# Layer 0's convolution stage of a two-layer diffusion trunk: a list scheduler's order on all engines, other tap numbers on GpSimd, seven projection tiles at other places

## The chip, the cores and the metric

The kernel runs on one core of a Trainium2 chip. The metric is the device time of one execution in microseconds (us); lower is better. Five queues run side by side and meet only at semaphores: TensorE (PE in the profile, its weight loads PEld), VectorE (DVE), ScalarE (ACT), GpSimd (POOL), and SyncE (SP), which here issues nearly all DMAs. Each works through its own instructions strictly in the order in which the program lists them: an instruction that waits holds up all that stand behind it on the same engine.

## The reference, cut to what matters

One inference step on 128 context tokens and 512 latent tokens (640 columns in the kernel, laid out with the channels on the partitions). Layer 0 is a Conformer convolution branch, layer 1 a bidirectional state-space branch. The change touches layer 0 alone:

```python
def conformer_branch(h, on_grid, w_in, b_in, w_dw, b_dw, ln_g, ln_b, w_out):
    u = h @ w_in + b_in
    a, a_gate, z = jnp.split(u, 3, axis=-1)
    v = a * jax.nn.sigmoid(a_gate)
    ...                                     # latent tokens: rows of 64 columns, each padded by itself
    v = depthwise_conv(v, w_dw, b_dw)       # 31 taps, padding 15
    v = jax.nn.silu(layer_norm(v, ln_g, ln_b))
    return (v * jax.nn.silu(z)) @ w_out
```

`w_in` is 1024 x 6144, so `a`, `a_gate` and `z` have 2048 channels each: 16 tiles of 128 channels each, 48 tiles in all. All arithmetic is in float32.

## The kernel before, in words

**Projection.** A tile of `u` is 128 channels by 640 columns in one PSUM buffer of two banks, 320 columns each. Each weight tile `wf` (512 KB) is split into a rounded part `wh` (ScalarE, L78) and the rest `wl` (GpSimd, L80), and so is the activation (`h_hi`, `h_lo`); a tile is the sum of three products over eight blocks of 128 inputs and two halves, 48 matmuls (`dense_all`, L157). There are two PSUM buffers for these products (`mm`), two buffers for `wf` and three each for `wh` and `wl`. Tiles are named a0 to a15, g0 to g15 (the gate) and z0 to z15 below. g0, a0 and g1 are made while the input is normalised; from 57 us on the stage makes a1, then g2, a2, g3, a3 and so on, z0 to z6 between them, and after the convolutions z7 to z15. In the profile a tile is called `u__` and a number: u__609 is a1, u__3811 is z6.

**Gate and convolution.** ScalarE takes the sigmoid of a g tile (L333), VectorE multiplies (L338, `v`). Item i of the convolution is channel tile i of `v`. Its centre tap is made by ScalarE into an accumulator `cva` in PSUM (L354, two of them), and 30 taps are left. Most are one VectorE instruction each (L361); the outermost ones, which are the shortest, are made by ScalarE as a product `tp` (L385, three buffers) that GpSimd adds (L390) to `cv`, the item's result in SBUF, once ScalarE has copied the accumulator there (L388). The context tokens are treated as two rows of 64 as well, and GpSimd adds what crosses the seam between them (L375, L377, L394). How many taps of an item go to ScalarE and GpSimd is a tuple of 16 numbers, 94 taps in all. For items 14 and 15 `cv` is cleared first and VectorE adds the accumulator last (L392).

**Sums beside it.** The layer norm needs the sums of `cv` and of its square over all channels. For items 0 to 9 they are made in a third kind of product, `side` (L190), which takes one of the two `mm` buffers, six items behind the gate; VectorE adds them up (L402). Items 10 to 15 go into one PSUM buffer `pst` later, and the statistics follow (L502 to L518). In the same `side` buffer 12 blocks of the adaLN parameters are multiplied (L111, weights `wa`, four DMAs of 256 KB per block), copied as a row by ScalarE (L117) and turned by TensorE in the spare columns of the next a tile (L122).

**After it.** z7 to z15 are multiplied, VectorE normalises the 16 items (L524, L525), gates them (L530), and the output projection `o` follows in three passes; layer 1 begins behind it.

**What sets the order.** In layer 0 the framework decides: it keeps the written order as a priority and issues on each engine what its own model of readiness lets it. Layer 1 has a list scheduler written in the kernel, the class `Order`: generators yield operations with an engine and a planned duration, keys (results) and rings (buffers), and `run` always issues the operation that can start earliest by its own clocks. Planned durations set the order and nothing else; on the chip the engines wait for semaphores.

Of the kernel before, what the change touches and what calls it, by code (L numbers as in the profile page):

```python
# [13 lines left out]
P = 128  # L14
NT = 640
# [26 lines left out]
def trunk(ctx: ExitStack, tc: tile.TileContext, a: dict):  # L42
# [190 lines left out]

    first = {}
# [57 lines left out]
    with tc.tile_pool(name="l0", bufs=1) as lp:  # L292
# [5 lines left out]
        LAG = 10  # L298


        Z_AT = {5: (0,), 10: (1,), 13: (2,), 14: (3, 4), 15: (5, 6)}
        Z_END = list(range(7, 16))
# [3 lines left out]
        order += [32 + j for j in Z_END]  # L306

# [23 lines left out]
        def sigmoid(i, psg):  # L331
            sg = tmp.tile([P, NT], F32, tag="tm", bufs=2, name="sg")
            S.activation(out=halves(sg), in_=psg[:, :, 0:HN], func=AF.Sigmoid, bias=c("b_in", 16 + i))  # L333
            return sg

        def gate(i, sg, psa):
            v = tmp.tile([P, NT], F32, tag="v", bufs=4, name="v")
            V.scalar_tensor_tensor(out=halves(v), in0=psa[:, :, 0:HN], scalar=c("b_in", i), in1=halves(sg), op0=ALU.add, op1=ALU.mult)  # L338
            return i, v

# [6 lines left out]
        def conv(items, npool, final=False):  # L347


            order = sorted((t for t in range(CK) if t != 15), key=lambda t: -abs(t - 15))  # L350
            late, taps = order[:npool], order[npool:]
            accs = [cvp.tile([P, 1024], F32, tag="cva", bufs=2, name="cva")[:, 0:NT] for _ in items]
            for (i, v), acc in zip(items, accs):
                S.activation(out=acc, in_=v, func=AF.Identity, scale=w_dw(i, 15), bias=c("b_dw", i))  # L354
                if final:
                    G.memset(cv[i], 0.0)
            for tap in taps:
                d = tap - 15
                lo, hi = max(0, -d), min(64, 64 - d)
                for (i, v), acc in zip(items, accs):  # L360
                    V.scalar_tensor_tensor(out=rows(acc)[:, :, lo:hi], in0=rows(v)[:, :, lo + d : hi + d], scalar=w_dw(i, tap), in1=rows(acc)[:, :, lo:hi], op0=ALU.mult, op1=ALU.add)  # L361
            for (i, v), acc in zip(items, accs):
                out = cv[i]

                e = eb[i % 3]
                S.copy(out=e[:, 0, 14:29], in_=v[:, HN : HN + 15])
                S.copy(out=e[:, 1, 0:15], in_=v[:, 49:64])
                oa = out[:, 49:64]
                seam = bass.AP(tensor=oa.tensor, offset=oa.offset, ap=[list(oa.ap[0]), [HN - 49, 2], [1, 15]])
                ea = e[:, :, :]  # L370
                win = bass.AP(tensor=ea.tensor, offset=ea.offset, ap=[list(ea.ap[0]), [30, 2], [1, 15], [1, 15]])
                wa = w_dw(i, 16)
                wv = bass.AP(tensor=wa.tensor, offset=wa.offset, ap=[list(wa.ap[0]), [-16, 2], [1, 15], [0, 15]])
                pr = lp.tile([P, 2, 15, 15], F32, tag="pr", bufs=1, name="seam")
                G.tensor_tensor(out=pr, in0=win, in1=wv, op=ALU.mult)  # L375
                for a0, a1, n in ((0, 8, 7), (0, 4, 4), (0, 2, 2), (0, 1, 1)):
                    G.tensor_add(out=pr[:, :, a0 : a0 + n, :], in0=pr[:, :, a0 : a0 + n, :], in1=pr[:, :, a1 : a1 + n, :])  # L377
                if final:
                    G.tensor_add(out=seam, in0=seam, in1=pr[:, :, 0, :])
                tps = []  # L380
                for tap in late:
                    d = tap - 15
                    lo, hi = max(0, -d), min(64, 64 - d)
                    tp = lp.tile([P, 10, 52], F32, tag="tp", bufs=3, name="tp")
                    S.activation(out=tp[:, :, 0 : hi - lo], in_=rows(v)[:, :, lo + d : hi + d], func=AF.Copy, scale=w_dw(i, tap))  # L385
                    tps.append((tp, lo, hi))
                if not final:
                    S.copy(out=out, in_=acc)  # L388
                for tp, lo, hi in tps:
                    G.tensor_add(out=rows(out)[:, :, lo:hi], in0=rows(out)[:, :, lo:hi], in1=tp[:, :, 0 : hi - lo])  # L390
                if final:
                    V.tensor_add(out=out, in0=out, in1=acc)  # L392
                else:
                    G.tensor_add(out=seam, in0=seam, in1=pr[:, :, 0, :])  # L394

        def ln_sums(i, ps):
            sq = tmp.tile([P, NT], F32, tag="tm", bufs=2, name="sq")
            S.activation(out=sq, in_=cv[i], func=AF.Square)
            for t, s in ((cv[i], 0), (sq, QN)):
                quarter_sums(ps[:, s : s + QN], t, True, True)  # L400
            if i:
                V.tensor_add(out=ssum, in0=ssum, in1=ps[:, 0 : 2 * QN].rearrange("p (a n) -> p a n", a=2))  # L402
# [1268 lines left out]
```

## Time and profile before

| | us |
|---|---|
| median of 3 runs | 1117.86 (1117.59 to 1118.91) |
| the profiled execution's own time | 1117.72 |
| its span, first to last instruction | 1115.9 |
| projection and convolution, a1 to z6 on TensorE | 57.2 to 368.5 |
| last addition of the convolution on VectorE | 387.8 |
| sums of items 10 to 15 added up | 396.6 |
| first output pass on TensorE ends | 471.4 |

The page gives the busy time of each engine and the costliest groups. The views used below: the windows (busy time of each engine between two times), the groups (engine, operation, `out<-in`, shape, count, busy time, mean of one, idle time before them and what ended it), the waits (who waited for whom, total, times, longest), the timeline (start, length, engine, line, and in brackets the idle time before and its releaser) and the chain of work that ended last (start, length, what). Matmuls overlap: a tile of 48 issues every 7.04 us.

### The profile page before, as it was taken

The numbers are of one execution on the slowest core, as the hardware profiler recorded it, in microseconds if no ns is written. First come the engines' busy times: TensorE is split into PE (matmuls) and PEld (weight loads), VectorE is DVE, ScalarE is ACT, GpSimd is POOL, SyncE is SP. The second block draws the span as 40 slices with busy tenths as digits, with TensorE's granted clock in tenths as the row PEclk, the third lists the DMA queues.
The fourth block names the chain that finished last, engine by engine and source line by source line (L and its number), as shares of the span: only waits on it lengthen the run. The fifth ranks groups of instructions, "written<-read, shape, count | busy, mean of one in ns | idle before, by whom it ended". The sixth has DMA issues, their size and how long they took to land.

```text
span 1115.9 us, 19084 instructions
## 1 busy us (share of the span) xinstructions
PE 1067.5 (96%) x7560; PEld 971.8 (87%) x7560; DVE 831.1 (74%) x1182; ACT 573.4 (51%) x994; POOL 493.3 (44%) x421
## 2 busy tenths in 40 slices
PE   6999999998998999899999999999999999999996
PEld 3898889797898999899989897899899888978896
DVE  2579999989899859623368978998766695777673
ACT  6544456455645356421266666584536472644442
POOL 1255797788778726600000046414541544254213
PEclk9999999999999999999999999999999999999997
DMA  9434224323321211432412274334343514343102
GB/s 362 166 118 147 95 95 133 111 85 126 101 68 60 77 48 38 146 110 67 142 40 95 72 156 117 87 103 115 86 115 104 118 63 114 104 114 87 57 20 94
DMA packets 79049, 115.95 MB, mean 104 GB/s; under 512 B 26096, under 2 KB 49008, under 8 KB 78960
## 3 DMA queue, kind: packets, MB, share of 16 engines
q1 hardware_dynamic: 78240, 113.91, 34.4%
q8 instruction: 59, 0.97, 0.4%
q10 hardware_dynamic: 720, 0.82, 0.2%
q14 instruction: 30, 0.25, 0.1%
HBM read 109.80 MB, written 4.92 MB: 103 GB/s over the span
## 4 chain that ended last, share of the span: by engine, by line
PE 71%; DVE 14%; ACT 6%; issue 3%; DMA 3%; POOL 1%; SPq 1%; POOLq 0%; DVEq 0%; ACTq 0%
PE pz L833 8%; PE o L833 8%; PE xs L833 6%; DVE cva L361 3%; PE o L1342 3%; PE po L1114 2%; PE pst L1051 2%; PE B L833 2%; PE py L1182 2%; DVE xs L875 2%; DVE cn L524 2%; ACT wh L78 2%; PE C L833 1%; PE o__5398 L148 1%; PE o__4929 L148 1%
## 5 line engine op out<-in xcount | busy, mean ns | idle before, releaser
L361 DVE SCALAR_TENSOR_TENSOR cva<-v,cst,cva 128x550 f32<-128x550 f32 (+12 forms) x386 | 286.0, 815 | 10.2 <-ACT cva L354 8.7
L80 POOL TENSOR_TENSOR wl<-wf,wh 128x1024 fp32r<-128x1024 f32 (+1 forms) x50 | 119.1, 2382 | 122.2 <-ACT wh L78 117.4
L78 ACT CAST wh<-wf 128x1024 fp32r<-128x1024 f32 (+1 forms) x75 | 71.5, 956 | 180.0 <-PE o__4929 L148 37.4
L390 POOL TENSOR_TENSOR cv<-cv,tp 128x490 f32<-128x490 f32 (+3 forms) x94 | 113.4, 1211 | 14.1 <-ACT cv L388 9.4
L795 ACT CAST wh<-wf 128x1024 fp32r<-128x1024 f32 x53 | 55.5, 1047 | 82.1 <-PE o L833 27.8
L799 DVE TENSOR_TENSOR wl<-wf,wh 128x1024 fp32r<-128x1024 f32 x51 | 69.2, 1357 | 32.9 <-ACT wh L795 32.4
L833 PE MATMUL o<-yhl,wh 128*128 128x320 f32 x384 | 92.1, 327 | 0.0
L385 ACT ACTIVATE tp<-v,cst 128x490 f32<-128x490 f32 (+3 forms) x94 | 65.8, 716 | 40.6 <-POOL cv L390 40.5
L833 PE MATMUL pz<-h_hi,wh 128*128 128x384 f32 (+1 forms) x256 | 84.6, 330 | 0.5 <-ACT up L862 0.5
L1120 POOL TENSOR_TENSOR y<-y,yo 128x512 f32<-128x512 f32 x32 | 44.7, 1397 | 80.9 <-DVE yo L1118 80.8
L833 PE MATMUL pz<-h_hi,wl 128*128 128x384 f32 (+1 forms) x256 | 79.1, 309 | 0.0
L833 PE MATMUL pz<-h_lo,wh 128*128 128x384 f32 (+1 forms) x256 | 79.0, 309 | 0.0
L833 PE MATMUL xs<-h_hi,wh 128*128 128x384 f32 (+1 forms) x224 | 77.4, 346 | 0.0
L80 DVE TENSOR_TENSOR wl<-wf,wh 128x512 fp32r<-128x512 f32 (+1 forms) x25 | 27.2, 1087 | 66.3 <-ACT wh L78 66.2
L833 PEld LDWEIGHTS o<-yhl,wh 128*128 128x128 f32 x384 | 63.9, 188 | 7.8 <-issue 7.8
L875 DVE SCALAR_TENSOR_TENSOR xs<-up,cst,xs 128x642 f32<-128x642 f32 x64 | 69.0, 1079 | 2.2 <-ACT xs L873 0.8
L833 PE MATMUL xs<-h_hi,wl 128*128 128x384 f32 (+1 forms) x224 | 69.3, 309 | 0.0
L833 PE MATMUL xs<-h_lo,wh 128*128 128x384 f32 (+1 forms) x224 | 69.2, 309 | 0.0
L833 PE MATMUL o<-yhl,wl 128*128 128x320 f32 x192 | 59.2, 309 | 0.0
L989 POOL TENSOR_TENSOR gb<-gb,cols 128x512 f32<-128x512 f32 x20 | 24.9, 1246 | 75.8 <-DMA gb<-acd 75.8
L995 ACT ACTIVATE gf<-gf,cols 128x128 f32<-128x128 f32 x160 | 49.8, 392 | 16.6 <-DVE gf L991 16.5
L628 POOL MEMSET up<- 128x2 f32 x2 | 0.2, 100 | 117.2 <-DVE h_lo L219 117.2
(685 smaller groups left out, 3406.7 us busy)
## 6 DMA issues: line engine op xcount, KB each, us to landing
wf<-w_in SPq DMA_DIRECT2D x48, 512.0 KB, 3.6
wa<-w_ada SPq DMA_DIRECT2D x64, 256.0 KB, 4.8
wf<-w_out SPq DMA_DIRECT2D x24, 512.0 KB, 3.7
wf<-w_xbc SPq DMA_DIRECT2D x24, 512.0 KB, 3.7
gf<-acd SPq DMA_DIRECT2D x40, 256.0 KB, 4.8
wa<-w_ada SPq DMA_DIRECT2D x16, 512.0 KB, 10.2
wf<-w_z SPq DMA_DIRECT2D x16, 512.0 KB, 3.8
gb<-acd SPq DMA_DIRECT2D x40, 128.0 KB, 4.7
```

The source lines that it names most:

```text
L78: S.copy(out=wh[:, :n], in_=wf[:, :n])
L80: sub.tensor_sub(out=wl[:, :n], in0=wf[:, :n], in1=wh[:, :n].bitcast(F32))
L361: V.scalar_tensor_tensor(out=rows(acc)[:, :, lo:hi], in0=rows(v)[:, :, lo + d : hi + d], scalar=w_dw(i, tap), in1=rows(acc)[:, :, lo:hi], ...
L385: S.activation(out=tp[:, :, 0 : hi - lo], in_=rows(v)[:, :, lo + d : hi + d], func=AF.Copy, scale=w_dw(i, tap))
L390: G.tensor_add(out=rows(out)[:, :, lo:hi], in0=rows(out)[:, :, lo:hi], in1=tp[:, :, 0 : hi - lo])
L795: S.copy(out=cell["wh"], in_=cell["wf"])
L799: e_.tensor_sub(out=cell["wl"], in0=cell["wf"], in1=cell["wh"].bitcast(F32))
L833: T.matmul(ps[:, b, at_ : at_ + t1 - t0], lhsT=w_, rhs=t_[:, t0:t1], start=k == 0 and n == 0, stop=k == nk - 1 and n == 2)
L875: t = yield op(VL, 0.89, lambda: V.scalar_tensor_tensor(out=acc, in0=u[:, d : d + PW], scalar=c("w_c", j * 5 + d), in1=acc, op0=ALU.mult, ...
L995: t = yield op(ACT, 0.39, lambda: S.activation(out=gv[:, h_, :], in_=gv[:, h_, :], func=AF.Exp, bias=cols1[ch][:, o8 + h_ : o8 + h_ + 1]), ...
L1120: t = yield op(PO, 1.29, lambda: G.tensor_add(out=y, in0=y, in1=yo))
L1342: T.matmul(ps, lhsT=wt, rhs=t_[:, tok], start=k == 0 and n == 0, stop=k == 3 and n == 2)
```

## The change

The class `Order` moves ahead of layer 0 unchanged but for its priorities, which it now takes as an argument, and layer 0's stage is written as generators for it. `PLAN0` is TensorE's order of a, g, z and side products (`s`); `NPOOL` the numbers of taps that go to ScalarE and GpSimd, 121 in all. Sums stand in the side product of their number, behind the ada block and ahead of the next a tile. Weight loads and the loads of the ada blocks are issued in the scheduler's order. The split of the first weight tile in `PLAN0` may go to VectorE and does; all others go to GpSimd. The buffer `tp` gets 54 columns a row instead of 52. The work itself is the same: 36 tiles in this stage, 12 blocks, 10 items' sums, 30 taps an item.

```diff
-        Z_AT = {5: (0,), 10: (1,), 13: (2,), 14: (3, 4), 15: (5, 6)}
-        order = [1]
-        for i in range(16):
-            order += [18 + i, 2 + i] * (i < 14) + [32 + j for j in Z_AT.get(i, ())]
...
-            conv([items[i]], (7, 6, 7, 6, 7, 6, 7, 6, 7, 6, 7, 6, 6, 4, 3, 3)[i], i >= 14)
...
+        PLAN0 = "a1 g3 s3 g2 s2 z0 a2 a3 z1 g5 g4 s4 s5 a4 a5 g6 s6 a6 g7 s7 a7 g8 s8 g9 a8 z2 z3 s9 a9 g10 s10 a10 g11 s11 a11 g12 s12 a12 g13 s13 a13 g14 s14 a14 g15 s15 a15 z4 z5 z6"
+        NPOOL = (10, 7, 9, 7, 6, 9, 11, 5, 4, 7, 10, 10, 10, 8, 4, 4)
...
+        def weights():
+            for m in tiles0 + order[:2]:
+                yield get("wf")
+                wf = gp.tile([P, 1024], F32, tag="wf", bufs=2, name="wf")
+                t = yield op(SP, 0.35, lambda: nc.sync.dma_start(out=wf, in_=a["w_in1"][m]))
+                start(split(m, wf), t)
+
+        def split(m, wf):
+            yield get("wh")
+            wh = gp.tile([P, 1024], F32R, tag="wh", bufs=3, name="wh")
+            yield op(ACT, 1.05, lambda: S.copy(out=wh, in_=wf))
+            yield get("wl")
+            wl = gp.tile([P, 1024], F32R, tag="wl", bufs=3, name="wl")
+            t = yield either((PO, 2.41, lambda: G.tensor_sub(out=wl, in0=wf, in1=wh.bitcast(F32))), (VL, 1.23, lambda: V.tensor_sub(out=wl, in0=wf, in1=wh.bitcast(F32))), bias=0.0 if m == tiles0[0] else 9.0)
...
+        def blocks():
+            for n, (l, b) in enumerate(BLOCKS):
+                if n > 1:
+                    yield key(("ada", n - 2))
+                for _ in range(4):
+                    yield get("cs")
+                blk = []
+                t = yield op(SP, 1.8, lambda: blk.append(ada_load(l, b, cs, 2)))
...
+        def filler():
+            blks = []
+            for name in plan:
+                i = int(name[1:])
+                if name[0] == "s":
+                    n = i - 2
...
+                    yield get("mm")
+                    ps = mm("side")
+                    if n < 12:
...
+                        t = yield op(PE, 1.07, sums_of_block)
...
+                    if i >= 6:
+                        j = i - 6
+                        yield key(("sq", j))
...
+                        t = yield op(PE, 0.78, sums)
...
+        def conv():
+            for i in range(16):
+                yield key(("init", i))
+                for tap in TAPS[NPOOL[i]:]:
+                    d, lo, hi = span_of(tap)
+                    t = yield op(VE, 0.24 + 0.01 * (hi - lo), lambda: V.scalar_tensor_tensor(out=rows64(accs[i], lo, hi), in0=rows64(vs[i], lo + d, hi + d), scalar=w_dw(i, tap), in1=rows64(accs[i], lo, hi), op0=ALU.mult, op1=ALU.add))
+                post(("taps", i), t)
+                start(copied(i), t) if i < 14 else start(last_add(i), t, "conv")
...
+        def seam_sums(i):
...
+            for n, tap in enumerate(TAPS[:NPOOL[i]]):
+                d, lo, hi = span_of(tap)
+                yield key(("tp", i, n))
+                t = yield op(PO, 1.12 if i < 14 else 1.3, lambda: G.tensor_add(out=rows64(cv[i], lo, hi), in0=rows64(cv[i], lo, hi), in1=sgs["tp", i, n][:, :, 0 : hi - lo]))
+                put("tp", t)
...
+        with tc.manual_schedule():
+            run.clock = [0.0, -3.0, -3.0, -3.0, -9.0]
...
+            start(weights(), -9.0)
+            start(after_g(0, first[0][1]), -1.8)
+            start(after_g(1, first[2][1]), 0.0)
+            start(blocks(), -9.0)
+            start(filler(), 0.0)
```

How it moves instructions, at the places that the prediction speaks of. **SyncE's queue as the stage begins**: `wf` are the weight tiles of `w_in`, the first of them a1's; `wa` with 1024 columns are the last blocks for the stage ahead, `wa` with 512 columns those of the side products, whose buffers lie where the stage ahead had its own. Before:

```order
L76 DMA wf_597<-w_in1 128x1024
L104 DMA wa_444<-w_ada 128x1024
L104 DMA wa_446<-w_ada 128x1024
L76 DMA wf_603<-w_in1 128x1024
L76 DMA wf_660<-w_in1 128x1024
L104 DMA wa_718<-w_ada 128x512
L104 DMA wa_720<-w_ada 128x512
L104 DMA wa_722<-w_ada 128x512
L104 DMA wa_724<-w_ada 128x512
L76 DMA wf_726<-w_in1 128x1024
```

Now:

```order
L104 DMA wa_444<-w_ada 128x1024
L104 DMA wa_446<-w_ada 128x1024
L104 DMA wa_592<-w_ada 128x512
L104 DMA wa_594<-w_ada 128x512
L104 DMA wa_596<-w_ada 128x512
L104 DMA wa_598<-w_ada 128x512
L470 DMA wf_589<-w_in1 128x1024
L104 DMA wa_603<-w_ada 128x512
L104 DMA wa_605<-w_ada 128x512
L104 DMA wa_607<-w_ada 128x512
L104 DMA wa_609<-w_ada 128x512
L470 DMA wf_601<-w_in1 128x1024
```

a1's weights stood ahead of the last loads of the stage before; they stand now behind the first four loads of the side blocks.

**ScalarE at the same place**: `u__253` is g0, `u__254` g1, `wh` a weight tile's rounded part. Before:

```order
L333 ACTIVATE sg<-u__253,cst_92 128x640
L78 CAST wh<-wf 128x1024 x2
L333 ACTIVATE sg<-u__254,cst_92 128x640
L366 COPY eb_581<-v 128x15
L367 COPY eb_581<-v 128x15
L385 ACTIVATE tp<-v,cst_92 128x10x49 x2
L385 ACTIVATE tp<-v,cst_92 128x10x50
L354 ACTIVATE cva<-v,cst_92 128x640
```

Now:

```order
L476 CAST wh<-wf 128x1024
L508 ACTIVATE sg<-u__253,cst_92 128x640
L508 ACTIVATE sg<-u__254,cst_92 128x640
L635 ACTIVATE cva<-v,cst_92 128x640
L674 ACTIVATE tp<-v,cst_92 128x10x49 x2
L476 CAST wh<-wf 128x1024
```

The cast of a1's weights (the first row now) stands ahead of the first sigmoid; before, a1's cast had been made long before this piece.

**TensorE between an a tile's neighbours**: before, the sums of an item (here item 1, `cv_976`) stood inside the a tile (a7, u__1712), with the ada block alone between g7 and a7.

```order
L157 MATMUL u__1712<-h_hi,wh 128x320
L157 MATMUL u__1712<-h_lo,wh 128x320
L190 MATMUL side<-cv_976,ones 32x160 x4
L190 MATMUL side<-sq,ones 32x160 x4
L157 MATMUL u__1712<-h_hi,wl 128x320
```

Now both products of the side buffer stand between g6 (u__1593) and a6 (u__1700):

```order
L496 MATMUL u__1593<-h_hi,wl 128x320
L587 MATMUL side<-wa,scz 32x256 x8
L190 MATMUL side<-cv_799,ones 32x160 x4
L190 MATMUL side<-sq,ones 32x160 x4
L496 MATMUL u__1700<-h_hi,wh 128x320
```

The work between the g and the a tile has grown by the sums, which have left the a tile.

**GpSimd through one item**: `wl` is the rest of a weight tile, `cv<-cv,tp` one tap of an item, `seam` the seam's sums. Before, item 4 (`cv_1562`), with some of item 5's rows:

```order
L80 TENSOR_TENSOR wl<-wf,wh 128x1024 x2
L390 TENSOR_TENSOR cv_1562<-cv_1562,tp 128x10x49 x2
L390 TENSOR_TENSOR cv_1562<-cv_1562,tp 128x10x50 x2
L80 TENSOR_TENSOR wl<-wf,wh 128x1024
L390 TENSOR_TENSOR cv_1562<-cv_1562,tp 128x10x51 x2
L390 TENSOR_TENSOR cv_1766<-cv_1766,tp 128x10x49
L390 TENSOR_TENSOR cv_1562<-cv_1562,tp 128x10x52
L390 TENSOR_TENSOR cv_1766<-cv_1766,tp 128x10x49
L394 TENSOR_TENSOR cv_1562<-cv_1562,seam 128x2x15
```

Now, item 11 (`cv_3203`):

```order
L709 TENSOR_TENSOR cv_3203<-cv_3203,seam 128x2x15
L479 TENSOR_TENSOR wl<-wf,wh 128x1024
L715 TENSOR_TENSOR cv_3203<-cv_3203,tp 128x10x49 x2
L715 TENSOR_TENSOR cv_3203<-cv_3203,tp 128x10x50 x2
L715 TENSOR_TENSOR cv_3203<-cv_3203,tp 128x10x51 x2
L479 TENSOR_TENSOR wl<-wf,wh 128x1024
L715 TENSOR_TENSOR cv_3203<-cv_3203,tp 128x10x52 x2
L715 TENSOR_TENSOR cv_3203<-cv_3203,tp 128x10x53 x2
L699 TENSOR_TENSOR seam<-eb_581,cst_92 128x450
```

The item has ten taps instead of seven, and the subtractions for the weight tiles stand between them as before.

More of the change, by code (lines that the diff above doesn't have):

```diff
@@ L345, in rows @@
             return t.rearrange("p (r w) -> p r w", w=64)
[L347 to L402, printed above, removed]
-            else:
-                V.tensor_copy(out=ssum, in_=ps[:, 0 : 2 * QN].rearrange("p (a n) -> p a n", a=2))
@@ L428, in gated @@
-        def gated(i):
-            psg = in_tile(16 + i)
-            sg = sigmoid(i, psg)
-            sd = side(i - 6)
-            psa = in_tile(i)
-            bias = turned(sd, psa)
-            item = gate(i, sg, psa)
-            bias()
-            return item
+        sz = [None] * 16
         def z_tile(j):
@@ L466, in trunk, with cst_w @@
+        late, loaded = [], []
+        del order[:2]
+        def cst_w(name):
+            return cs(name)
         worder = []
```

432 lines of the change are left out of this document (296 added, 136 removed).

## The prediction

> **What bounds the kernel now.** I read the page's totals first, then the windows from stage to stage, the chain of waits, and the engines' waits inside the stage.
>
> ```profile
> span 1115.9 us, 19084 instructions
> 57.20:368.30 311.10, 292.13 (x2129) 271.59 (x2130) 285.45 (x403) 160.09 (x250) 236.94 (x220) 0.99 0.32 104
> 368.30:396.50 28.20, 28.20 (x258) 25.93 (x256) 19.06 (x25) 11.63 (x15) 18.11 (x16) 1.00 0.19 58
> 396.50:471.40 74.90, 72.26 (x473) 71.14 (x473) 57.68 (x60) 42.61 (x60) 39.78 (x22) 0.98 0.27 85
> 57.23 7.30 PE u__609 L157 x48
> 64.54 7.04 PE u__666 L157 x48
> 352.58 8.83 PE u__3754 L157 x48
> 361.41 7.04 PE u__3811 L157 x48
> 396.09 0.41 PE pst L190 x8
> ```
>
> The windows give the length, then busy time of PE, PEld, DVE, ACT, POOL. From a1 (u__609, at 57.2) to the end of z6 (u__3811, at 368.5) TensorE is idle for 19.0 of 311.1 us, VectorE for 25.7. From 352.6 to the last sums of `pst` at 396.5 the chain runs on TensorE alone, without a gap. Behind that comes a stretch of 74.9 us, in which VectorE normalises, until the first output pass ends at 471.4. So what the change can win must bring TensorE to `pst` earlier, with the convolution ready there in time.
>
> What TensorE's work alone would take, by these rows:
>
> ```profile
> 85.59 1.07 PE L111 MATMUL side<-wa,scz 128*32 128x256 f32 x16
> 163.12 0.48 PE L190 MATMUL side<-cv,ones 128*32 128x160 f32 x8
> 163.42 0.46 PE L190 MATMUL side<-sq,ones 128*32 128x160 f32 x8
> 166.69 0.50 PE L122 MATMUL u__1712<-cst,ada_row 128*128 128x2 f32 x4
> 167.05 0.39 PE L157 MATMUL u__1773<-h_hi,wh 128*128 128x320 f32 x1
> ```
>
> 36 tiles x 7.04 = 253.4; 12 ada blocks x 1.07 = 12.8; 10 sums x 0.74 (to the end of the second) = 7.4; 12 turns x 0.36 (166.69 to the next tile at 167.05) = 4.3: 278 us, ending at 335. It ends 33 us later now. That is the most that the order can win.
>
> ```profile
> PE u__3754 L157 <- ACT sz L441: 2.8, 1, 2.8
> PE side L111 <- DMA wa<-w_ada: 2.8, 6, 0.7
> PE u__2845 L157 <- DVE ssum L402: 2.2, 1, 2.2
> PE u__922 L157 <- ACT sg L333: 0.7, 1, 0.7
> 386.99 0.82 DVE L392 TENSOR_TENSOR cv<-cv,cva 128x640 f32<-128x640 f32 x1
> ```
>
> The waits are many and small: 0.7 us ahead of an a tile, because the sigmoid of the g tile frees its buffer later than the short side product ends, and a few of 2 us and more; behind the 2.81 us wait the tile took 8.83 instead of 7.04. VectorE's last addition ends at 387.8, 8.7 us before `pst` ends: now the convolution isn't the last to arrive, TensorE is.
>
> **The change part by part.** *Side products.* With sums and ada block together ahead of the a tile, 1.07 + 0.74 = 1.8 us stand there, and u__922 began 1.8 us after g3 ended (85.6 to 87.4). So the 0.7 us waits go, as do the two long ones if their cause (a late z sigmoid, late sums) is gone: the plan's order is worth up to those 33 us if nothing else is late.
>
> *Start.* SyncE's queue holds what speaks against it.
>
> ```profile
> 25.50 0.33 SPq L76 DMA_DIRECT2D wf<-w_in  x1
> 56.97 1.75 SPq L104 DMA_DIRECT2D wa<-w_ada  x4
> 60.64 37.87 SPq L76 DMA_DIRECT2D wf<-w_in  x7
> 56.39 0.80 ACT L333 ACTIVATE sg<-u__253,cst 128x640 f32<-128x640 f32 x1 [2.16 <-PE u__253 L148]
> 61.66 0.89 ACT L354 ACTIVATE cva<-v,cst 128x640 f32<-128x640 f32 x1
> 64.94 1.06 ACT L78 CAST wh<-wf 128x1024 fp32r<-128x1024 f32 x1 [2.38 <-DMA wf<-w_in]
> 62.59 1.57 DVE L361 SCALAR_TENSOR_TENSOR cva<-v,cst,cva 128x520 f32<-128x520 f32 x2 [4.49 <-ACT cva L354]
> 471.39 1.24 DVE wl L80
> wf<-w_in SPq DMA_DIRECT2D x48, 512.0 KB, 3.6
> ```
>
> Before, a1's load was issued at 25.50. The four `wa` loads that now stand ahead of it went out only at 56.97, when the stage ahead had let go of the memory that they overwrite. Behind them a1's load is issued at 58.7. Alone it lands 3.6 later, at 62.3; the load behind the same four `wa` landed at 64.9. I take 64.2, nearer to the second, since the same megabyte is ahead of it. Queued behind it on ScalarE are the cast (1.06) and then both sigmoids, on VectorE the subtraction (1.24), which stands ahead of the first gate; the first gate and through it the whole convolution wait for them. TensorE begins a1 at 64.2 + 1.06 + 1.24 + 0.4 for the hand-overs = 66.9, 9.7 us later than at 57.2 (7.8 to 10.4 by the two landings). After such a wait the first tile is slow as u__3754 was: 1.8. So TensorE ends z6 at 335 + 11.5 = 346.5 at the earliest, 22 us earlier than now. The gate starts behind the subtraction (66.7, 0.9), then the accumulator (0.9): VectorE's first tap moves from 62.6 to 68.7. Two weight loads fewer in the loading stage ahead may bring 57.2 forward: 0 to 1.5, taken as 0.5.
>
> *Taps.* 27 taps go from VectorE to ScalarE and GpSimd.
>
> ```profile
> L361 DVE SCALAR_TENSOR_TENSOR cva<-v,cst,cva 128x550 f32<-128x550 f32 (+12 forms) x386 | 286.0, 815 | 10.2 <-ACT cva L354 8.7
> L390 POOL TENSOR_TENSOR cv<-cv,tp 128x490 f32<-128x490 f32 (+3 forms) x94 | 113.4, 1211 | 14.1 <-ACT cv L388 9.4 <-ACT tp L385 1.5
> L80 POOL TENSOR_TENSOR wl<-wf,wh 128x1024 fp32r<-128x1024 f32 x40 | 96.2, 2407 | 57.0 <-ACT wh L78 52.2 <-PE side L111 4.6
> L377 POOL TENSOR_TENSOR seam<-seam 128x210 f32<-128x210 f32 (+1 forms) x64 | 26.2, 409 | 2.9
> L375 POOL TENSOR_TENSOR seam<-eb,cst 128x450 f32<-128x450 f32 x16 | 15.6, 972 | 0.9
> L390 POOL TENSOR_TENSOR cv<-cv,tp 128x520 f32<-128x520 f32 x6 | 7.8, 1307 | 0.2
> L385 ACT ACTIVATE tp<-v,cst 128x490 f32<-128x490 f32 (+3 forms) x94 | 65.8, 716 | 40.6 <-POOL cv L390 40.5
> L388 ACT COPY cv<-cva 128x640 f32<-128x640 f32 x14 | 9.6, 686 | 13.7 <-DVE cva L361 13.7
> ```
>
> VectorE: 27 x 286.0/386 = 20 us less, 266 for taps; with gates, sums and additions (some 20 us, its other busy time) it could end near 355 from its first tap at 68.7; the third item's a2 stands fifth in the plan (66.9 + 1.8 + 5 x 7.04 + sides 3 = 107), so it stands still for some 6 us there: 361. ScalarE gains 27 x 0.716 = 19 us and had 160 of 311 busy: covered. GpSimd: 96.2 for 40 subtractions up to the last tap, 113.4 + 27 x 1.307 (the added taps are the wider ones) = 148.7, seams 26.2 + 15.6 + 5 for the small rest: 295 us. Some 12 of it (four subtractions, a seam) fits ahead of the first tap, which waits for item 0's 20 taps and its copy: 68.7 + 20 x 0.741 + 0.9 + 0.7 = 85. That ends at 85 + 283 = 368 without a single wait. It had 311.1 - 236.9 = 74 us without work before, nearly all slack; now it has none to spare, so its waits for VectorE's copies and ScalarE's casts count: 0 below, 20 above (a quarter of those 74). I take 6, since its backlog hides most: 374. **GpSimd becomes the last to arrive**: last addition 0.8, square and sums 1.5, hand-overs and two z evacuations ahead on ScalarE 3: 380 for the end of `pst`. TensorE alone would be there at 346.5 + 31 (z7 to z10 with their `pst` parts, 28.2 now to one tile less) = 377.5. So 396.5 becomes 380, and behind a TensorE that had to wait there the matmuls ahead of the statistics cost 1.5 more.
>
> The diff plans 1.12 us for such an addition. [...]
>
> *Behind it* (396.5 to 471.4, 74.9 us, and the rest) the order of normalisation, output passes and layer 1 stays nearly the same, so the whole shift is kept. Sum: 16.5 - 1.5 + 0.5 = 15.5 earlier, bounds 7 (GpSimd waits 20, `pst` at 389) and 22 (no waits, landing at 62.3, 1.5 at the head). The profiled execution took 1117.72, 1.8 around its span and 0.14 under the median: 1117.7 - 15.5 = 1102.
>
> **The rivals.** *No late start and no late GpSimd* (the first loads are released earlier than at 56.97, and a tap costs as planned): TensorE runs at its own pace, `pst` ends at 366, 30 us earlier: 1088. For it: the plan starts SyncE 9 us early. Against: the release at 56.97, the 1.211. *The plan's order doesn't fit*: GpSimd's additions, 0.1 to 0.2 us longer than planned, push its waits over 20 us and tap, cast and sigmoid queue behind each other; `pst` ends at 390 to 396: 1114. For it: 295 us in a window of 310. Against: a plan that is late everywhere by the same amount loses it once. *Slower*: GpSimd's subtractions arrive late tile after tile. They stand in its queue among ten taps in a row; from g10 on a lateness of 2.5 us ahead of a tile costs 2.5 and the slow tile behind it, 1.8. From 6 such tiles on the gain at TensorE is gone (346.5 + 6 x 4.3 = 372); with 10 of the last 16, 389 there, 21 us late: 1138. For it: GpSimd full. Against: three buffers of `wh` and `wl`, so that it works some 8 us ahead.
>
> [...]
>
> **How the numbers follow.** Forecast 0.63 (its own range 1096 to 1111), TensorE's pace 0.15, order that doesn't fit 0.13, slower 0.09. The range is to hold 8 in 10: 1090 to 1112 leaves out the slower case, half of the third and the low edge of the second. A run of this kernel can tell about 0.2%, 2.2 us, from no change. Faster: 0.63 + 0.15 + most of the third (0.10) = 0.88; the same 0.03; slower 0.09.
>
> **What would show it.** Right: TensorE idle for some 10 us ahead of a1, waiting for a subtraction on VectorE behind a DMA; the waits ahead of the a tiles gone; GpSimd over nine tenths busy from 85 to 370; its last tap near 374, `pst` at 380; the stretch behind it 75 us long. Wrong: a1 at 57 (then the first rival), GpSimd idle while VectorE or TensorE waits for ScalarE (the second), z6 ending behind 360 (the third), or a stretch behind `pst` that has grown by what was won.

## The result and the profile after

The changed kernel takes 1132.8 us (1132.4 to 1133.9), the kernel before 1117.8: ratio 1.0133, interval 1.0116 to 1.0149. It is 15 us slower; 1102 was forecast, with 1090 to 1112 as the range. The windows of the changed kernel (length; busy time of PE, PEld, DVE, ACT, POOL with counts; granted clock; DMA):

```profile
span 1132.1 us, 19153 instructions
57.20:66.40 9.20, 0.00 (x0) 0.00 (x0) 0.69 (x1) 1.77 (x3) 0.00 (x0) 0.66 0.89 297
66.40:386.40 320.00, 292.31 (x2129) 278.49 (x2130) 297.44 (x383) 175.93 (x274) 265.21 (x243) 0.96 0.30 97
386.40:417.50 31.10, 31.10 (x282) 29.66 (x280) 15.02 (x18) 12.88 (x17) 20.48 (x17) 1.00 0.24 78
```

TensorE waits 9.2 us ahead of a1, then needs 320.0 us for the 36 tiles that took 311.1, and ends z6 at 386.4 instead of 368.5. The share that stands out is VectorE's: 297 of 320 us busy, with 27 taps fewer. The group of its taps now (count, busy time, mean of one, idle time ahead of them; the prediction shows the one before), and the chain that ended last, before and then now, in shares of the span:

```profile
L643 DVE SCALAR_TENSOR_TENSOR cva<-v,cst,cva 128x560 f32<-128x560 f32 (+11 forms) x359 | 294.7, 824 | 20.3 <-ACT cva L635 9.0
PE pz L833 8%; PE o L833 8%; PE xs L833 6%; DVE cva L361 3%; PE o L1342 3%; PE po L1114 2%; PE pst L1051 2%; PE B L833 2%; PE py L1182 2%; DVE xs L875 2%; DVE cn L524 2%; ACT wh L78 2%; PE C L833 1%; PE o__5398 L148 1%; PE o__4929 L148 1%
DVE cva L643 19%; PE pz L1012 8%; PE o L1012 8%; PE xs L1012 5%; POOL cv L715 3%; PE o L1521 3%; PE po L1293 2%; PE pst L1230 2%; PE B L1012 2%; PE py L1361 2%; DVE xs L1054 2%; DVE cn L813 2%; PE C L1012 1%; PE o__5453 L148 1%; PE o__4982 L148 1%
```

VectorE's taps (`DVE cva`) are 19% of that chain now and were 3% before: the taps now set the pace of the stage. Before, 386 taps kept VectorE busy for 286.0 us, 0.741 each; now 359 keep it busy for 294.7, 0.821 each, and the 11 us of idle time that no other engine explains lie between them as well. The instruction itself is hardly longer (824 ns against 815; the widest are left). What differs is whether a tap overlaps the one ahead. VectorE's timeline, before and then after:

```profile
257.20 10.97 DVE L361 SCALAR_TENSOR_TENSOR cva<-v,cst,cva 128x520 f32<-128x520 f32 x15 [0.62 <-ACT cva L354]
```

```profile
275.69 8.55 DVE L643 SCALAR_TENSOR_TENSOR cva<-v,cst,cva 128x610 f32<-128x610 f32 x10
366.91 33.49 DVE L643 SCALAR_TENSOR_TENSOR cva<-v,cst,cva 128x570 f32<-128x570 f32 x39
400.31 0.82 DVE L663 TENSOR_TENSOR cv<-cv,cva 128x640 f32<-128x640 f32 x1
407.62 0.82 DVE L663 TENSOR_TENSOR cv<-cv,cva 128x640 f32<-128x640 f32 x1 [6.50 <-POOL cv L715]
417.56 0.49 DVE L791 TENSOR_TENSOR ssum<-ssum,pst 128x320 f32<-128x320 f32 x1 [9.12 <-PE pst L190]
```

0.73 us a tap before, 0.86 after. Over the neighbouring taps of each trace (those over 1 us apart, behind waits, left out) the mean from start to start is 0.738 us before and 0.855 after. Of 355 such neighbours before, 315 begin some 0.09 us ahead of the end of the one in front; of 333 now, 320 begin 0.035 us behind it. By the widths below, the first are taps behind another item's, the second taps behind one of their own item. In the order of VectorE's queue the widths show what stands where. Before (a later item's narrow taps between the wide ones of the item ahead), and now:

```
L361 SCALAR_TENSOR_TENSOR cva<-v,cst_92,cva 128x10x53
L361 SCALAR_TENSOR_TENSOR cva<-v,cst_92,cva 128x10x57
L361 SCALAR_TENSOR_TENSOR cva<-v,cst_92,cva 128x10x54
L361 SCALAR_TENSOR_TENSOR cva<-v,cst_92,cva 128x10x58
```

```
L643 SCALAR_TENSOR_TENSOR cva<-v,cst_92,cva 128x10x56 x2
L643 SCALAR_TENSOR_TENSOR cva<-v,cst_92,cva 128x10x57 x2
L643 SCALAR_TENSOR_TENSOR cva<-v,cst_92,cva 128x10x58 x2
```

Before, the framework took taps of two items in turn. The new generator `conv` yields all taps of an item, one behind the other, and each reads the accumulator that the one ahead has just written. The scheduler's clocks let it start 0.08 us before that one's end (`OVER`), chained or not. I call this the chain below: 359 x 0.117 = 42 us, of which the wider taps make 359 x 0.009 = 3.

The start came at the time that was forecast. ScalarE and VectorE as the stage begins:

```profile
64.63 1.04 ACT L476 CAST wh<-wf 128x1024 fp32r<-128x1024 f32 x1 [11.95 <-DMA wf<-w_in]
65.70 1.23 DVE L479 TENSOR_TENSOR wl<-wf,wh 128x1024 fp32r<-128x1024 f32 x1 [12.17 <-ACT wh L476]
66.85 0.88 DVE L517 SCALAR_TENSOR_TENSOR v<-u__102,cst,sg 128x640 f32<-128x640 f32 x1
68.74 1.60 DVE L643 SCALAR_TENSOR_TENSOR cva<-v,cst,cva 128x540 f32<-128x540 f32 x2 [1.02 <-ACT cva L635]
```

And TensorE's waits ahead of a tiles and side products haven't gone; they have grown (total, times, longest), with ScalarE's queue at one of the two worst a tiles:

```profile
PE u__615 L496 <- ACT sg L508: 10.3, 1, 10.3
PE side L587 <- ACT sz L529: 4.8, 1, 4.8
PE u__1888 L496 <- ACT sg L508: 3.6, 1, 3.6
PE u__2662 L496 <- ACT sg L508: 3.6, 1, 3.6
ACT tp L674 <- POOL cv L715: 69.9, 66, 4.9
```

```profile
186.03 0.73 ACT L674 ACTIVATE tp<-v,cst 128x510 f32<-128x510 f32 x1 [1.26 <-POOL cv L715]
187.28 0.71 ACT L674 ACTIVATE tp<-v,cst 128x490 f32<-128x490 f32 x1 [0.52 <-POOL cv L715]
187.90 0.77 ACT L508 ACTIVATE sg<-u__1777,cst 128x640 f32<-128x640 f32 x1
```

g7 (u__1777) was done at 183.4, but its sigmoid stands behind products `tp` that wait for a buffer from GpSimd. So the sigmoid starts at 187.9, and a7 (u__1888) 3.6 us late. I take GpSimd to be late because VectorE hands over the items late (over the stage it waits 18.9 us for copies of VectorE's accumulators); for this one wait no run shows it.

### The profile page after: what moved, and what is told of

Its sections match the earlier page's. It is cut to its first block, busy times and chain, and to the rows that moved or that the text cites. A ratio compares the mean times of both kernels' runs of the same rounds, so it can differ in the third digit from the quotient of the medians.

```text
span 1132.1 us, 19153 instructions
## 1 busy us (share of the span) xinstructions
PE 1066.7 (94%) x7560; PEld 980.1 (87%) x7560; DVE 834.0 (74%) x1156; ACT 590.5 (52%) x1019; POOL 519.3 (46%) x447
## 4 chain that ended last, share of the span: by engine, by line
PE 55%; DVE 30%; POOL 5%; ACT 3%; issue 3%; DMA 2%; SPq 1%; POOLq 0%; DVEq 0%; ACTq 0%
DVE cva L643 19%; PE pz L1012 8%; PE o L1012 8%; PE xs L1012 5%; POOL cv L715 3%; PE o L1521 3%; PE po L1293 2%; PE pst L1230 2%; PE B L1012 2%; PE py L1361 2%; DVE xs L1054 2%; DVE cn L813 2%; PE C L1012 1%; PE o__5453 L148 1%; PE o__4982 L148 1%
## 5 line engine op out<-in xcount | busy, mean ns | idle before, releaser
L643 DVE SCALAR_TENSOR_TENSOR cva<-v,cst,cva 128x560 f32<-128x560 f32 (+11 forms) x359 | 294.7, 824 | 20.3 <-ACT cva L635 9.0
L715 POOL TENSOR_TENSOR cv<-cv,tp 128x490 f32<-128x490 f32 (+5 forms) x121 | 144.2, 1192 | 7.6
L674 ACT ACTIVATE tp<-v,cst 128x490 f32<-128x490 f32 (+5 forms) x121 | 86.1, 722 | 69.9 <-POOL cv L715 69.9
L479 POOL TENSOR_TENSOR wl<-wf,wh 128x1024 fp32r<-128x1024 f32 x37 | 89.0, 2405 | 26.0 <-ACT wh L476 26.0
L78 ACT CAST wh<-wf 128x1024 fp32r<-128x1024 f32 (+1 forms) x37 | 31.9, 862 | 86.1 <-PE o__4984 L148 35.2
```

The lines of the kernel that those rows point to most:

```text
L78: S.copy(out=wh[:, :n], in_=wf[:, :n])
L479: t = yield either((PO, 2.41, lambda: G.tensor_sub(out=wl, in0=wf, in1=wh.bitcast(F32))), (VL, 1.23, lambda: V.tensor_sub(out=wl, in0=wf, ...
L643: t = yield op(VE, 0.24 + 0.01 * (hi - lo), lambda: V.scalar_tensor_tensor(out=rows64(accs[i], lo, hi), in0=rows64(vs[i], lo + d, hi + d), ...
L674: t = yield op(ACT, 0.72, lambda: S.activation(out=tp[:, :, 0 : hi - lo], in_=rows64(vs[i], lo + d, hi + d), func=AF.Copy, scale=w_dw(i, t ...
L715: t = yield op(PO, 1.12 if i < 14 else 1.3, lambda: G.tensor_add(out=rows64(cv[i], lo, hi), in0=rows64(cv[i], lo, hi), in1=sgs["tp", i, n] ...
```

## The experiments

The last of the z tiles, z15, ends at 438.9 us before and at 456.2 after; from there TensorE is busy for 657 of the last 677 us before and of the last 676 now, and in all the runs below with a table the time is the end of z15 plus 679 us, within 3 us. So the tables give both. Theory A is the chain, B the late start, C GpSimd's additions, longer than planned, that hold up ScalarE and TensorE.

**Undoing one thing at a time.** First the taps in turn again, in the changed kernel:

```diff
-                        wait = MARGIN[eng] if ch[5] != eng else -OVER[eng]
+                        wait = MARGIN[eng] if ch[5] != eng else -self.over[eng]
+        run.over = {**OVER, VE: -0.04}
-        def conv():
-            for i in range(16):
+        def conv(first):
+            for i in range(first, 16, 2):
-            start(conv(), 0.0)
+            start(conv(0), 0.0)
+            start(conv(1), 0.0)
```

> The changed kernel with the convolution's taps on VectorE drawn from two items in turn (one generator for the even items, one for the odd), and the scheduler told that a tap can't start before the end of the tap that wrote the same accumulator. Theory A (chained taps: a tap that reads the accumulator that the tap right ahead of it wrote starts 0.855 us after it, 0.738 where another item's tap stands ahead, so VectorE sets the end): start to start falls to 0.74, the taps' busy time from 294.7 to about 263, VectorE's last addition from 408 to about 375, pst ends near 385, and the time is 1098 to 1108, with GpSimd the last to arrive. Theory B (the 9 us late start is the loss): VectorE's order doesn't matter, 1128 to 1133. Theory C (GpSimd's additions of 1.19 against the 1.12 planned hold up ScalarE behind the three tp buffers, and through the sigmoids TensorE): the waits for sigmoids stay, 1125 to 1133.

Then the weights' priority (`"weights": 4` to `-2` in `PRIO0`), the numbers of taps (`NPOOL` as before), and, in the kernel before, the chain alone:

> The changed kernel with the weight loads ahead of the ada blocks' loads in the scheduler's priorities, so that a1's load no longer stands behind the four wa loads. All theories: a1 starts at 57 to 58 instead of 66.4. Theory A: VectorE's first tap comes about 6 us earlier and VectorE works without a pause from there, so the end comes 4 to 6 us earlier: 1127 to 1129. Theory B: TensorE's 10 us and the slow first tile are the loss, 1118 to 1122. Theory C: hidden by the later waits, 1131 to 1133.

> The changed kernel with the numbers of taps of before (94 instead of 121 on ScalarE and GpSimd). Theory A: VectorE has 27 taps more at 0.83 each, some 22 us, the last addition near 430: 1150 to 1156, although GpSimd has 32 us less to do. Theory B: 1131 to 1135. Theory C: GpSimd is relieved, the sigmoids are on time: 1112 to 1125.

```diff
+                    if tapped:
+                        tc.add_manual_dep(ins.ins, tapped[-1], ..., reason="order")
+                    tapped.append(ins.ins.name)
```

> The kernel before with one thing changed: VectorE's taps of an item stand behind all taps of the item ahead of it, where before taps of two items stood in turn. Theory A: 386 taps x 0.117 = 45 us more on VectorE; its idle time in the stage (25.7) and the 8.7 us between its last addition and the sums cover part, so 11 to 36 us are left, taken as 28: 1146 (1129 to 1154), and VectorE becomes the last to arrive. Theories B and C: both are about things that only the changed kernel has, so 1117 to 1120.

| | us | ratio to before (interval) | z15 ends |
|---|---|---|---|
| before, taps chained | 1146.3 | 1.0247 (1.0218 to 1.0277) | 469.8 |
| changed, taps in turn | 1122.1 | 1.0036 (1.0022 to 1.0050) | 442.2 |
| changed, weights first | 1129.9 | 1.0099 (1.0067 to 1.0131) | 452.4 |
| changed, 94 taps | 1142.6 | 1.0218 (1.0190 to 1.0246) | 462.7 |

The first line is the cleanest: the edit asks for nothing but another order of VectorE's taps, and the kernel before loses 28 us, as theory A had it. It isn't quite alone: the framework then puts ScalarE's and GpSimd's queues in another order too (GpSimd's additions of two items no longer stand mixed), and what that is worth was not measured. Its taps:

```profile
L363 DVE SCALAR_TENSOR_TENSOR cva<-v,cst,cva 128x560 f32<-128x560 f32 (+11 forms) x386 | 315.2, 820 | 16.7 <-ACT cva L356 4.5
```

315.2 us busy instead of 286.0, for the same 386 instructions. With 94 taps on GpSimd the changed kernel gets slower, by 10 and not by 22 us, so the sign is A's and C falls; the size isn't. GpSimd's relief may give some of it back; that is not shown. Taps in turn win 11 us where I expected some 30: another queue takes over. VectorE's end in that run:

```profile
358.10 22.36 DVE L645 SCALAR_TENSOR_TENSOR cva<-v,cst,cva 128x510 f32<-128x510 f32 x29 [2.34 <-ACT cva L637]
394.49 0.82 DVE L665 TENSOR_TENSOR cv<-cv,cva 128x640 f32<-128x640 f32 x1 [14.03 <-POOL cv L717]
407.42 0.82 DVE L665 TENSOR_TENSOR cv<-cv,cva 128x640 f32<-128x640 f32 x1 [6.82 <-POOL cv L717]
```

VectorE now waits 20.8 us for GpSimd's last taps. All but six of its own are done at 380.5, GpSimd's last at 407.4. The weights' priority won 3 us; it brought a1 to 56.9 but the first tap only to 66.4: a1's load is early, the next tile's still stands behind four `wa`, and its cast stands ahead of the first accumulator in ScalarE's queue.

**The start and GpSimd's share.** Each weight load as a chain of its own, so that the first two go ahead of all side blocks, and 109 taps instead of 121:

```diff
-        def weights():
-            for m in tiles0 + order[:2]:
-                yield get("wf")
+        def weight(m):
+            yield get("wf")
...
+            for m in tiles0 + order[:2]:
+                start(weight(m), -9.0)
-        NPOOL = (10, 7, 9, 7, 6, 9, 11, 5, 4, 7, 10, 10, 10, 8, 4, 4)
+        NPOOL = (10, 7, 9, 7, 6, 9, 11, 5, 4, 7, 10, 8, 7, 5, 2, 2)
```

> The kernel with taps in turn, and 12 taps fewer for ScalarE and GpSimd in the last five items (109 instead of 121). Theory D (with the taps in turn GpSimd is the last to arrive: its last tap ended at 407.4 while VectorE had its own taps behind it at 381 and waited 20.8 us for the two last additions): GpSimd has 12 x 1.26 = 15 us less, VectorE 12 x 0.8 = 10 us more, both arrive near 391, pst ends 14 us earlier: 1108 (1104 to 1112). Rival E (TensorE's waits for the z sigmoids and ScalarE's casts set the end): 1118 to 1123.

> The kernel with taps in turn, and the loads of the first two weight tiles issued ahead of all side blocks' loads (each load a chain of its own in the scheduler, so that it doesn't wait for the landing of the one before). a1 starts at 57 and VectorE's first tap at 62 to 63 instead of 68. Theory D: GpSimd, the last to arrive, starts its taps 5 us earlier and is never ahead of its work, so the end comes 4 to 6 us earlier: 1117 (1115 to 1119). Rival: the last four items' lateness is made behind 370 by the subtractions for z7 to z11 in GpSimd's queue alone, 1120 to 1123.

> Both: taps in turn, first weights early, 109 taps for GpSimd. Theory D: the gains add up, 14 and 5 us: 1103 (1098 to 1108), under the kernel before. If TensorE or ScalarE take over as the last to arrive: 1108 to 1114.

> Taps in turn, first weights early, 115 taps for GpSimd: between 121 (1110.3; VectorE waited for GpSimd) and 109 (1104.4; VectorE's taps ended 9 us behind GpSimd's). If the two engines' balance sets the end, 1100 to 1104; if TensorE does, 1104 to 1108.

> The changed kernel with the first two weight tiles' loads ahead of all side blocks' loads, taps chained as in the changed kernel. Theory A: VectorE's first tap comes at 59 instead of 68.7 and VectorE works without a pause from there, so the end comes 8 to 10 us earlier: 1123 to 1125. If the start is hidden by GpSimd's lateness: 1128 to 1132.

| changed kernel with | us | ratio to before (interval) | z15 ends |
|---|---|---|---|
| in turn, 109 taps | 1113.1 | 0.9944 (0.9926 to 0.9961) | 435.2 |
| in turn, first weights early | 1110.3 | 0.9926 (0.9900 to 0.9951) | 432.6 |
| in turn, early, 115 taps | 1108.2 | 0.9913 (0.9881 to 0.9945) | 429.1 |
| in turn, early, 109 taps | 1104.4 | 0.9872 (0.9843 to 0.9902) | 426.1 |
| chained, early | 1123.5 | 1.0054 (1.0037 to 1.0071) | 445.8 |

The start is worth 9.3 us with the taps chained (VectorE's first tap at 57.8), as expected, and 11.8 with the taps in turn, twice what I expected. Fewer taps win 9.0 (I expected 14) and, on top of the early start, 5.9. Between 121 and 109 no optimum shows.

**The taps' numbers alone, in the kernel before**, where the framework sets the order:

```diff
-            conv([items[i]], (7, 6, 7, 6, 7, 6, 7, 6, 7, 6, 7, 6, 6, 4, 3, 3)[i], i >= 14)
+            conv([items[i]], (10, 7, 9, 7, 6, 9, 11, 5, 4, 7, 10, 10, 10, 8, 4, 4)[i], i >= 14)
-                    tp = lp.tile([P, 10, 52], F32, tag="tp", bufs=3, name="tp")
+                    tp = lp.tile([P, 10, 54], F32, tag="tp", bufs=3, name="tp")
```

> The kernel before with the changed numbers of taps alone (121 on ScalarE and GpSimd instead of 94), its order by the framework, in which taps of two items stand in turn. By the sums of the prediction: VectorE has 20 us less, GpSimd 33 us more of its 74 without work, TensorE's order is the same and sets the end: 1117 (1114 to 1120). If GpSimd's subtractions come late to TensorE behind the added taps: 1124 to 1135. If VectorE set the end before: 1105 to 1112.

> The kernel before with 121 taps on ScalarE and GpSimd and VectorE's taps of an item behind all taps of the item ahead of it: what the change does to taps and chain, without its order for the other engines and without its start. Theory A: 359 x 0.117 = 42 us more on VectorE, whose own taps ended at 365 with TensorE's tiles z7 to z15 and GpSimd's last taps (395) behind; some 30 of it is covered at the end, so VectorE's taps end near 403 and the time is 1105 + 10 to 25, taken as 1122: the numbers of taps then gain little or nothing over before. If the changed kernel's order on TensorE and ScalarE is what costs: 1105 to 1110.

> The kernel before with 109 taps on ScalarE and GpSimd (those of alternate_fewer). With 121 VectorE waited 29 us for GpSimd's last taps, but TensorE went from z6 (353) to z15 without a pause. Theory F (TensorE is the bound there again, and its waits in the stage are VectorE's lateness): VectorE has 9 us more to do ahead of the a tiles of the last items, TensorE ends 0 to 4 us later, GpSimd's 15 us less are not on the path: 1104 to 1109. If GpSimd's last taps set the end: 1092 to 1100.

> The kernel before with 103 taps on ScalarE and GpSimd. With 109 VectorE's last addition ended at 373 and GpSimd's last tap at 364, TensorE went from z6 (354) to z15 without a pause. If TensorE is the bound from 109 to 121, 103 is where VectorE's lateness comes back: 1103 to 1109. If VectorE's last addition still sets the end at 109: 1107 to 1112.

| kernel before with | us | ratio to before (interval) | z15 ends |
|---|---|---|---|
| 121 taps | 1105.2 | 0.9876 (0.9840 to 0.9911) | 423.5 |
| 121 taps, chained | 1133.3 | 1.0138 (1.0111 to 1.0166) | 456.1 |
| 109 taps | 1103.0 | 0.9878 (0.9848 to 0.9908) | 423.8 |
| 103 taps | 1111.4 | 0.9944 (0.9927 to 0.9960) | 431.8 |

This I had wrong, though one of the three ranges named it (VectorE as the bound, 1105 to 1112): the numbers of taps alone make the kernel 14 us faster. TensorE with 121 taps, the 36 tiles from a1 to z6, and VectorE's taps:

```profile
57.40:353.10 295.70, 285.13 (x2130) 268.34 (x2131) 273.19 (x384) 171.09 (x270) 250.46 (x228) 1.00 0.35 109
L361 DVE SCALAR_TENSOR_TENSOR cva<-v,cst,cva 128x540 f32<-128x540 f32 (+12 forms) x359 | 267.9, 819 | 8.6 <-ACT cva L354 7.1
```

The same tiles take 295.7 us instead of 311.1. TensorE's idle time fell from 19.0 to 10.6, and its busy time from 292.1 to 285.1: the two stretches of half clock in this stage of the kernel before (at 268.3 and 353.6, 3.4 us each) have gone too. VectorE is the only engine that got less work, so in the kernel before it was VectorE that held TensorE up, although each wait was short. One way is visible: the 2.2 us that TensorE waited for VectorE's sums (u__2845 <- `ssum`) have no counterpart with 121 or 109 taps, and with 103, where z15 comes 8 us later than with 109, a wait of 2.4 us for `ssum` is back. From 109 on VectorE's or GpSimd's end doesn't matter: with 121 VectorE's last addition comes 23 us later than with 109 (396.2 against 373.3), and z15 ends at the same time. With the taps chained on top, 1133.3: the changed kernel's time, without its order on TensorE and SyncE.

**What in a chained tap costs.** Each tap as two halves of five rows; once the two halves of a tap as neighbours, once all first halves of an item ahead of its second halves.

```diff
+                    for r in (0, 5):
-                    ... out=rows64(accs[i], lo, hi), ...
+                        ... out=rows64(accs[i], lo, hi)[:, r : r + 5], ...
```

> The changed kernel with each of VectorE's taps made as two instructions of five rows each, one half behind the other: neighbours write the same accumulator, but not the same rows. By the widths (0.751 us for 510 elements, 0.879 for 630) a half should take about 0.50 us. If a tap waits for the result of the tap ahead (dependence): neighbours are free of each other, start to start is about 0.08 under the duration, 0.42. If the accumulator's memory is what costs (same PSUM tile, whatever the rows): start to start is 0.03 above the duration, 0.53. The time is no matter here (VectorE gets 359 more instructions: 1135 to 1180).

> The same halves, but all first halves of an item ahead of its second halves, so that each instruction reads what the one right ahead of it wrote. By both explanations start to start is 0.03 above the duration, 0.53, and the time is above that of half_taps by 0.11 x 718 = up to 79 us if dependence is the cause, equal if the memory is.

They took 1233 and 1251 us (one run each; their plans differ elsewhere too, so the taps' spacing is compared and not the totals). VectorE's timeline of the first and of the second:

```profile
136.47 13.58 DVE L644 SCALAR_TENSOR_TENSOR cva<-v,cst,cva 128x285 f32<-128x285 f32 x24
```

```profile
133.55 7.94 DVE L643 SCALAR_TENSOR_TENSOR cva<-v,cst,cva 128x285 f32<-128x285 f32 x14
```

0.566 and 0.567 us a half, some 0.035 behind the end of the one ahead in both. So the rows don't decide: neighbours that share an accumulator but no row pay as much. In both, though, every half but the first of its item (702 of 718) waits for a semaphore that VectorE itself raises, and the traces don't keep for which value; if it is set by the accumulator and not by the rows, each half still waits for the one right ahead. Whether this wait costs, or the accumulator's memory, stays open; taking away the wait alone wasn't tried.

## Why the prediction was wrong, by its steps

- *VectorE: "27 x 286.0/386 = 20 us less, 266 for taps".* This is the first step that failed. The 0.741 us of that row is the price of a tap with another item's tap ahead of it, and I took it to an order that has none. VectorE needed 294.7 us and 11 us of gaps: 40 us more than the 266. The order of its queue, which shows the widths in turn before and in pairs now, was there to be read; the working draws on those of the other four engines alone. No rival had VectorE as the bound. The slower one (1138) had the sign and not the mechanism: no tile waited for a subtraction on GpSimd. Yet this step is not the whole miss: with the taps in turn the changed kernel takes 1122.1, still 20 us over the forecast. The second step that failed is GpSimd's waits, below.
- *What bounds the kernel now: TensorE, which ends "33 us later now. That is the most that the order can win".* No run here won more than 15 us. And TensorE's long waits came from VectorE's lateness more than from the plan's order, as the 121 taps alone show: there the waits of 0.7 us for sigmoids behind the short side products are as before, and the two longest, 2.8 and 2.2, are gone. Before, the 2.8 stood behind a copy on ScalarE that followed VectorE's taps (they ended at 351.1, the tile began at 352.6), the 2.2 behind VectorE's sums. I judged VectorE by its last addition, 8.7 us ahead of `pst`; the ends of items and the sums in the middle of its queue were what came late.
- *Start: a1 9.7 us late at 66.9, VectorE's first tap at 68.7.* Right: 66.4 and 68.7, with the load and the cast about as given. What a1 waited for last was not the subtraction, though, but g0's sigmoid, which stands behind the cast on ScalarE and frees the buffer (65.58 + 0.79 = 66.4; the subtraction ended at 66.9). Undone, it is worth 9 to 12 us; I had priced it as no part of the end, since GpSimd was to set that.
- *The waits ahead of the a tiles go.* Wrong: they grew to 3.6 us, behind `tp` products that wait for GpSimd. That is the mechanism of the rival in which the order doesn't fit. The chain is only part of its cause: with the taps in turn the longest such wait is still 3.0 us (a6, `PE u__1692 L498 <- ACT sg L510`).
- *GpSimd: 121 additions, 295 us, last tap at 374, `pst` at 380.* The durations held:

```profile
L715 POOL TENSOR_TENSOR cv<-cv,tp 128x490 f32<-128x490 f32 (+5 forms) x121 | 144.2, 1192 | 7.6
```

  1.192 us each and 0.06 between them, not the 1.12 planned. The sum was added up wrong: its terms make 291.7, not 295, so 280 from 85 on instead of 283. The end did not hold, and this is the second step that failed: the last tap came at 407.6 and `pst` at 417.5. Even with the taps in turn the last tap was at 407.4, and there GpSimd's work from 85 on was the 280 that was counted, 278, but it stood still for 44 us where I allowed 6, and 20 at most. Of those, 23.2 us are waits for ScalarE's casts and 7.9 for its copies, while ScalarE, in whose queue the casts stand among the products `tp`, waited 82.4 us for GpSimd to give back `tp` buffers and twice over 6 us for TensorE to give back a `wh`. How these waits lead to each other was not taken apart; that they come to 44 us and not to 6 is what the run shows. (The bound for 20 us of waits was too kind as well: 368 + 20 + 6 puts `pst` at 394, not 389.) The window of that run:

```profile
85.00:407.40 322.40, 304.54 (x2304) 292.63 (x2306) 272.63 (x376) 180.20 (x275) 278.05 (x253) 0.98 0.30 97
```

- *Behind `pst` the whole shift is kept.* Not quite: `pst` is 21 us later, z15 17.3, and the time grew by 15.0. It is z15's end that the time follows, not `pst`: with 121 taps in the old order VectorE's last addition came at 395 instead of 387, and the kernel still was 14 us faster:

```profile
395.34 0.82 DVE L392 TENSOR_TENSOR cv<-cv,cva 128x640 f32<-128x640 f32 x1 [8.69 <-POOL cv L390]
```

The account of the 15 us, along one path of measured kernels: the taps' numbers -14 (1105.2 against 1119.4 for before in that comparison), the chain +28 (to 1133.3, with what the framework moved along with it), and the new order with its late start nothing that shows (1132.8). In that nothing two things cancel: with the start undone but the taps chained, the scheduler's order takes 1123.5, 10 us less than the framework's with 121 chained taps. With the taps in turn that gain is gone: 1110.3 against 1105.2 with 121 taps, and with 109 the ratios are 0.9872 and 0.9878. These last two, 1104.4 with the scheduler's order (chain, start and twelve taps undone) and 1103.0 with the framework's, are the fastest kernels here, 1.2% under the one before.

## What to carry to other kernels

A mean duration from a profile holds for the order in which it was taken (here 0.741 us a tap in turn, 0.821 in a row): ahead of using it for a new order, look at what stands right ahead of the instruction in its queue, on the engines that look idle too. A scheduler that gives every instruction of an engine the same overlap sees no harm in a row of instructions on one accumulator (here 0.855 us from start to start instead of 0.738), so give it that price and let it draw from two chains. And an engine whose last work is early (here VectorE's, 8.7 us ahead of `pst`) can still hold up another in the middle of its queue (27 taps fewer made the kernel 14 us faster); to find out, take work off it alone and see whether the time moves.

## What the runs showed of the hardware

A tap on VectorE, 500 to 630 elements a partition in PSUM, started 0.035 us behind the end of a tap on the same accumulator (320 of 333 neighbours in the changed kernel) and some 0.09 ahead of the end of one on another (315 of 355 in the kernel before): 0.12 us of 0.85. The kernel before and the one with its taps chained have 386 taps each: 286.0 and 315.2 us busy, 28 us apart in time. So the number of operations isn't all that counts.

TensorE's clock fell behind a wait of 1.89 us and not behind one of 1.87. In the changed kernel, the first matmuls of a13 (u__3243) and of a12 (u__3051), and the windows of both tiles:

```profile
318.95 0.41 PE L496 MATMUL u__3243<-h_hi,wh 128*128 128x320 f32 x1 [1.89 <-ACT sg L508]
319.67 0.47 PE L496 MATMUL u__3243<-h_lo,wh 128*128 128x320 f32 x1
319.94 0.47 PE L496 MATMUL u__3243<-h_hi,wl 128*128 128x320 f32 x1
300.74 0.41 PE L496 MATMUL u__3051<-h_hi,wh 128*128 128x320 f32 x1 [1.87 <-ACT sg L508]
301.43 0.31 PE L496 MATMUL u__3051<-h_lo,wh 128*128 128x320 f32 x1
301.57 0.31 PE L496 MATMUL u__3051<-h_hi,wl 128*128 128x320 f32 x1
318.90:327.70 8.80, 8.75 (x50) 8.75 (x50) 8.48 (x12) 4.12 (x7) 8.25 (x10) 0.81 0.19 61
300.70:308.00 7.30, 7.26 (x50) 7.26 (x51) 7.02 (x11) 3.60 (x6) 7.07 (x6) 1.00 0.23 69
```

Behind 1.89 us of waiting the matmuls soon issue every 0.27 us (granted clock 0.81 over the tile), behind 1.87 every 0.145 (1.00). The length of the wait alone doesn't decide. The trace's clock records show more: in the two traces, before and after, the 12 lower stretches that the trace's end doesn't cut last 3.41 us (10 of them), 6.83 and 10.24, and in each trace all begin and end on one grid of 3.41 us steps that takes no notice of the tiles. The steps of that grid in which the two waits lie, each with the step behind it:

```profile
316.18:319.59 3.41, 1.52 (x28) 1.11 (x21) 3.30 (x5) 2.79 (x4) 3.17 (x5) 1.00 0.48 148
319.59:323.00 3.41, 3.41 (x15) 3.41 (x14) 3.30 (x6) 1.23 (x3) 3.17 (x5) 0.50 0.02 5
299.11:302.52 3.41, 1.78 (x12) 1.78 (x13) 3.30 (x6) 3.22 (x5) 2.23 (x3) 1.00 0.08 34
302.52:305.94 3.42, 3.42 (x25) 3.42 (x24) 3.31 (x5) 0.73 (x1) 3.42 (x3) 1.00 0.03 7
```

The 1.89 us lie in one step, in which TensorE is idle for 55%, and the next step has half the clock; the 1.87 us are cut by the grid, their step is idle for 48%, and the clock stays. Between 20 us and the last 20 us of the two traces, before and after, every step with TensorE idle for more than half (14 of them) is followed by a step at half clock, and only one with less is (25%, at 579 us of the changed kernel, in layer 1). Up to 48% idle, the other steps of these two kept it. In the traces of the other runs the limit was less sharp: a step idle for 53% kept the clock, some with 37 to 48% lost it, in layer 1 some with 24 to 35%. So no threshold follows, and why stays open.
